# Up projection's transpose: from TensorE to transposing DMAs with 16-bit halves taken apart and put together on POOL

## Chip, core and metric

The kernel runs as one program on one core of a Trainium2 chip. The metric is the device time of one execution in microseconds. A core has five engines that each run their own list of instructions in order: PE (TensorE, matrix products and transposes), ACT (ScalarE), DVE (VectorE), POOL (GpSimd) and SP (SyncE, which here issues DMAs). Sixteen DMA engines move data between HBM and the on-chip memory SBUF, and within SBUF. PE writes its results to a second on-chip memory, PSUM.

## What is computed

One layer of a decoder trunk, for 256 tokens of width 2048 in fp32. Mixed state-space and attention heads come first, then a feed-forward part, then a gated embedding. The change lies in the feed-forward part:

```python
u = _rmsnorm(h, ffn_norm_g[i]) @ w_up[i]            # 256 x 2048 times 2048 x 11264
u = _causal_dwconv(u, ffn_conv_w[i], ffn_conv_b[i]) # 3 taps along the tokens, per feature
g_ff, u_ff = jnp.split(u, [D_FF], axis=-1)          # D_FF = 5632
h = h + (jax.nn.silu(g_ff) * u_ff) @ w_down[i]
```

The convolution runs along the tokens, each feature with its own three weights and bias.

## The kernel before

**Products.** All large products have the same shape. `gemm` (line 221) walks over loads of 128 x 1024 weights (two slices of 128 input features by 512 output features, 512 KB). `load_w` (line 196) loads one with a DMA on SP's queue (line 205) into one of five buffers `w`; `split` (line 188) makes a high part `wh` with a cast on ACT (line 190) and the remainder `wl` with a subtraction on DVE (line 191), each into one of four buffers. `products` (line 209) then issues, for each of the two slices and each of the two blocks of 128 tokens, three matmuls of 128 x 128 by 512 (lines 217 to 219: high by high, high by low, low by high), so 12 matmuls for a load; in the last load of a product all of the first block of tokens comes first. The result, two PSUM tiles `acc` of 128 tokens x 512 features, comes from a ring of two pairs.

**Up projection.** `up(c)` (line 769) computes 512 features from eight loads. ACT evicts both `acc` tiles with the tokens' norm factor as scale into `u` (line 775; one tile per block of tokens, two buffers each). In `u` tokens lie on the partitions, while the convolution wants features there and tokens along the row. So `conv_chunk` (line 270) transposes: for each of four groups of 128 features and each of two token blocks PE multiplies a 128 x 128 piece by the identity (line 277), eight transposes per call, into PSUM tiles `tr`. `conv_tile` (line 261) then writes the last tap and the bias with ACT (line 264) and adds the two other taps with DVE (line 266), from `tr` into `cv`, an SBUF tile of 128 features x 4 x 256 tokens. `conv_chunk` has other callers in the state-space part; they keep it.

**Feed-forward loop.** 22 calls of `up`, in segments of pairs: `SEGS = [2, 2, 2, 2, 2, 1]`. For each pair: `up` for the gate, SiLU on it (ACT, line 789), `up` for the other half, the product of both on POOL (line 791), and a split of it into `gh` and `gl` (ACT and DVE, lines 190 and 191), which is the stationary operand of the down projection. After each segment `project` (line 371) runs the down projection of the segment before (four groups of 512 output features, two loads per pair each), and DVE adds its result to the residual (line 357). So a segment's `gT` is read by PE only after the next segment's up projections, and for the last segment after the down projection of the one before.

**Order of the work.** No order is written by hand. The program is traced in the order of the code, and a scheduler puts each engine's instructions into a fixed list at build time, playing through a timeline (`schedule_with_timeline_sim=True`, line 884). On the chip each engine runs its list in order and stops at the first instruction whose semaphore isn't there. DMAs that are issued from ACT stand in ACT's list.

Of the kernel before, what the change touches and what calls it, by code (L numbers as in the profile page):

```python
# [11 lines left out]
F32 = mybir.dt.float32  # L12
F32R = mybir.dt.float32r
I32 = mybir.dt.int32
AF = mybir.ActivationFunctionType
ALU = mybir.AluOpType
AX = mybir.AxisListType
# [2 lines left out]
P = 128  # L20
T = 256
# [4 lines left out]
NC = 512  # L26
# [38 lines left out]
def hybrid_layer(  # L65
# [20 lines left out]
    nc = tc.nc  # L86
    V, S, G, PE = nc.vector, nc.scalar, nc.gpsimd, nc.tensor
# [12 lines left out]
    def nm(s):  # L100
        uid[0] += 1
        return f"{s}_{uid[0]}"
# [2 lines left out]

    def sb(pool, shape, tag, dt=F32, bufs=None):
        kw = {} if bufs is None else {"bufs": bufs}
        size = math.prod(shape[1:]) * (2 if dt == mybir.dt.bfloat16 else 4)
        tags = sizes.setdefault(pool.id, {})
        tags[tag] = max(tags.get(tag, 0), -(-size // 32) * 32 * (bufs or pool.bufs))  # L110
        return pool.tile(shape, dt, tag=tag, name=nm(tag), **kw)
# [10 lines left out]
    def tr_tile():  # L122
        return ps_tr.tile([P, NC], F32, tag="tr", name=nm("tr"))
# [14 lines left out]
    def load_first(k, pieces=1):  # L138

        xt = sb(xin, [P, T], "xt", bufs=6)  # L140
        nc.sync.dma_start(xt, xT[:, k, :])
        w = sb(wp, [P, KW, NC], "w", bufs=WR)
        n = KW // pieces
        for c in range(0, KW, n):
            cs = slice(c, c + n)
            nc.sync.dma_start(w[:, cs, :], w_in[cs, k // KW, :, (k % KW) * NC : (k % KW + 1) * NC].rearrange("c p n -> p c n"))
        return w, xt
# [30 lines left out]
    g_attn, g_ffn, g_ple, g_ssm = (gn[:, i * KT : (i + 1) * KT] for i in range(4))  # L178
    posi = sb(const, [P, NB], "posi", I32)

    def rstd(ss, n, cols, tag):
        t = sb(small, [P, cols], "rs_t")
        V.tensor_scalar(t, ss, 1.0 / n, EPS, op0=ALU.mult, op1=ALU.add)
        r = sb(small, [P, cols], tag)
        G.tensor_tensor(out=r, in0=t, in1=nhalf[:, :cols], op=ALU.pow)
        return r

    def split(src, hi, lo, scale=None):
# [3 lines left out]
        else:  # L192
            S.activation(out=hi, in_=src, func=AF.Copy, scale=scale)
            V.scalar_tensor_tensor(out=lo, in0=src, scalar=scale, in1=hi.bitcast(F32), op0=ALU.mult, op1=ALU.subtract)
# [48 lines left out]
    def transpose_split(src, lhs, k0, gain=None):  # L243

        for half in range(2):
            tr = tr_tile().rearrange("p (a t) -> p a t", a=2)
            for i in range(2):
                f = half * 2 + i
                for b in range(NB):
                    PE.transpose(tr[:, i, b * P : (b + 1) * P], src[b][:, f * P : (f + 1) * P], ident)  # L250
            k = k0 + half * 2
            if gain is None:
                h, l = lhs.t[k // KG]
                j = k % KG
                split(tr, h[:, j : j + 2, :], l[:, j : j + 2, :])
            else:
                for i in range(2):
                    h, l = lhs.part(k + i)
                    split(tr[:, i, :], h, l, gain[:, k + i : k + i + 1])

    def conv_tile(ps, dst, taps, bias):

        n = len(taps)
        S.activation(out=dst, in_=ps, func=AF.Identity, scale=taps[n - 1], bias=bias)  # L264
        for s in range(1, n):
            V.scalar_tensor_tensor(  # L266
                out=dst[:, s:], in0=ps[:, : T - s], scalar=taps[n - 1 - s], in1=dst[:, s:], op0=ALU.mult, op1=ALU.add
            )

    def conv_chunk(src, dst, cw, ntap, c0):  # L270

        for half in range(2):
            tr = tr_tile().rearrange("p (a t) -> p a t", a=2)
            for i in range(2):
                f = half * 2 + i
                for b in range(NB):
                    PE.transpose(tr[:, i, b * P : (b + 1) * P], src[b][:, f * P : (f + 1) * P], ident)  # L277
            for i in range(2):
                f = half * 2 + i
                w = cw[:, (c0 + f) * (ntap + 1) : (c0 + f + 1) * (ntap + 1)]  # L280
                conv_tile(tr[:, i, :], dst[:, f, :], [w[:, j : j + 1] for j in range(ntap)], w[:, ntap : ntap + 1])
# [14 lines left out]
    with xin_:  # L296
        wd = sb(xin, [P, KT, 32], "wd")
        dhl = sb(xin, [P, KT, 64], "dhl", F32R)
        for k in range(KT):
            w, xt = first[k] if k < len(first) else load_first(k)  # L300
# [23 lines left out]
            if k in (5, 9):  # L324
                b = k // 4 - 1
                nc.sync.dma_start(hres[b], x[b])
                xs = sb(xin, [P, D], "xs")
                S.activation(out=xs, in_=hres[b], func=AF.Square, accum_out=ssx[:, b : b + 1])
        rx_ = rstd(ssx, D, NB, "rx_")
# [16 lines left out]
    def evac_scaled(acc, pool, tag, bufs=None):  # L346
        res = []
        for b in range(NB):
            t = sb(pool, [P, NC], f"{tag}{b}", bufs=bufs)
            S.activation(out=t, in_=acc[b], func=AF.Copy, scale=rx[:, b : b + 1])  # L350
            res.append(t)
        return res
# [6 lines left out]
    def next_lhs(lhs, ss, n, gain):  # L359

        for b in range(NB):
            sq = sb(small, [P, NC], "hsq")
            S.activation(out=sq, in_=hres[b][:, n * NC : (n + 1) * NC], func=AF.Square, accum_out=ss[:, b, n : n + 1])
        transpose_split([hres[b][:, n * NC : (n + 1) * NC] for b in range(NB)], lhs, 4 * n, gain)
# [17 lines left out]
    with tc.tile_pool(name="ssd", bufs=1) as sp, tc.tile_pool(name="dram", bufs=1, space=bass.MemoryType.DRAM) as dp:  # L382
        BT = sb(sp, [P, 4, T], "BT")
        CT = sb(sp, [P, 4, T], "CT")
        for c, (acc, dst) in enumerate(((acc_b, BT), (acc_c, CT))):
            t = evac_scaled(acc, sp, "ct", 1)
            conv_chunk(t, dst, scw, 4, 16 + 4 * c)
            S.activation(out=dst, in_=dst, func=AF.Silu)

# [9 lines left out]
        dt = sb(sp, [P, 64], "dt")  # L399
# [128 lines left out]
        with tc.tile_pool(name="rope", bufs=1) as rp:  # L528
# [3 lines left out]
            for j in range(HALF):  # L532
                f = float(np.float32(THETA) ** np.float32(-2.0 * j / ROPE))
# [62 lines left out]
    with tc.tile_pool(name="att_s", bufs=2) as as_, tc.tile_pool(name="att", bufs=2, reuse_waits="tile") as ap_:  # L596
# [5 lines left out]
        def norm_rope(acc, b, gain, tag):  # L602
            r = sb(ap_, [P, NC], "qkr", bufs=1)
            S.activation(out=r, in_=acc[b], func=AF.Copy, scale=rx[:, b : b + 1])
            n = sb(ap_, [P, NC], "qkn")
            S.activation(out=n, in_=r, func=AF.Square)
            ss = sb(as_, [P, 8], "ss8")
            V.tensor_reduce(out=ss, in_=v3(n, 8), axis=AX.X, op=ALU.add)
            rs = rstd(ss, HD, 8, "rs8")
            V.tensor_tensor(out=v3(r, 8), in0=v3(r, 8), in1=bc(rs, HD), op=ALU.mult)  # L610
            G.tensor_tensor(out=v3(n, 8), in0=v3(r, 8), in1=gain.unsqueeze(1).to_broadcast([P, 8, HD]), op=ALU.mult)
            n3 = v3(n, 8)
            a, c_ = n3[:, :, :HALF], n3[:, :, HALF:ROPE]
            cs = cos_t[:, b, :].unsqueeze(1).to_broadcast([P, 8, HALF])
            sn = sin_t[:, b, :].unsqueeze(1).to_broadcast([P, 8, HALF])
            t = [sb(as_, [P, 8, HALF], f"rot{i}", bufs=1) for i in range(4)]
            for i, (u_, w_) in enumerate(((a, cs), (c_, sn), (c_, cs), (a, sn))):
                G.tensor_tensor(out=t[i], in0=u_, in1=w_, op=ALU.mult)
            G.tensor_tensor(out=a, in0=t[0], in1=t[1], op=ALU.subtract)
            G.tensor_tensor(out=c_, in0=t[2], in1=t[3], op=ALU.add)  # L620
            return n
# [88 lines left out]
        for b in range(NB):  # L710
            n = norm_rope(acc, b, kg_, "k")
# [31 lines left out]
    fcw = sb(pp, [P, 88 * 4], "fcw")  # L743
# [23 lines left out]
    with tc.tile_pool(name="ffn", bufs=2) as fp:  # L767

        def up(c):
            acc = acc_pair()  # L770
            gemm(acc, hT, [w_up[c, g] for g in range(KT // KW)])
            t = []
            for b in range(NB):
                u_ = sb(fp, [P, NC], f"u{b}")
                S.activation(out=u_, in_=acc[b], func=AF.Copy, scale=rh[:, b : b + 1])
                t.append(u_)
            cv = sb(fp, [P, 4, T], f"cv{c // NPAIR}")
            conv_chunk(t, cv, fcw, 3, 4 * c)
            return cv

        pair = 0
        pending = []
        ssg = sb(small, [P, NB, 4], "ssg", bufs=1)

        for s, np_ in enumerate(SEGS):
            gT = Lhs(fp, KG * np_, "g")
            for i in range(np_):
                cg = up(pair + i)
                S.activation(out=cg, in_=cg, func=AF.Silu)
                cu = up(NPAIR + pair + i)  # L790
                G.tensor_tensor(out=cg, in0=cg, in1=cu, op=ALU.mult)  # L791
                split(cg, gT.t[i][0], gT.t[i][1])
            if pending:
                project(*pending.pop())
            pending.append((gT, w_down, pair, np_))
            pair += np_
        h2T = Lhs(act, KT, "a")
        project(*pending.pop(), lambda n: next_lhs(h2T, ssg, n, g_ple))
        embed()
# [88 lines left out]
```

## Time and profile before

| | us |
|---|---|
| median of three runs | 1484.79 |
| lowest and highest | 1484.22 and 1485.33 |
| the profiled execution | 1485.15 |
| its span, first to last instruction | 1483.4 |

The granted TensorE clock is 1.000 over the span. Busy time is given for PE (matmuls), PEld (PE's weight loads, which overlap PE), DVE, ACT and POOL. Matmuls are pipelined, so their durations overlap: the time of one is read from start to start. A row of a group of instructions gives line, engine, operation, output and inputs by name, shapes and count, then total busy time and mean ns of one, then the idle time of the engine ahead of them and what ended it. A row of the timeline gives start, length, engine, line and operation; in brackets stands the idle time ahead of it and what ended it. A row that ends in x2 or x4 merges neighbours. A row of the waits gives who waited for whom, us in total, times, and the longest. For one line, durations are given as min/median/max in ns.

### The profile page before, as it was taken

How to read it: one execution, taken by the hardware profiler on the slowest of the kernel's cores; microseconds unless marked ns; L12 is line 12 of the kernel's file. 1: busy time of each engine (PE TensorE's matmuls, PEld its weight loads, DVE VectorE, ACT ScalarE, POOL GpSimd, SP SyncE). 2: the span in 40 equal slices, each digit the busy share in tenths (PEclk: the TensorE clock that was granted, in tenths of full speed). 3: DMA queues.
4: the chain of work that ended last, by engine and by line, in shares of the span. 5: the costliest groups of instructions: out<-in, count | busy, mean ns of one | idle time of the engine just before them, and what ended most of it. 6: DMA issues, size and time to landing. Idle time of an engine off the chain costs nothing.

```text
span 1483.4 us, 18448 instructions
## 1 busy us (share of the span) xinstructions
PE 1472.3 (99%) x6836; PEld 1198.2 (81%) x6836; DVE 970.7 (65%) x1288; ACT 795.2 (54%) x1103; POOL 122.5 (8%) x120
## 2 busy tenths in 40 slices
PE   9999999999999999999999999999999999999998
PEld 6787888888777777788888888888888888888887
DVE  6668876756758687766556646565665556566854
ACT  6575555545555554566555545544543554454643
POOL 0002010024033030000000000000000000000000
PEclk9999999999999999999999999999999999999999
DMA  9665665655555555466666666666666666666673
GB/s 324 198 195 177 206 189 161 182 155 172 156 156 148 165 147 159 133 194 201 183 187 186 186 193 183 187 192 192 180 192 191 182 194 186 187 190 188 205 225 98
DMA packets 79433, 271.65 MB, mean 183 GB/s; under 512 B 9008, under 2 KB 11888, under 8 KB 78960
## 3 DMA queue, kind: packets, MB, share of 16 engines
q1 hardware_dynamic: 78912, 270.01, 60.1%
q8 instruction: 53, 0.87, 0.3%
q10 hardware_dynamic: 432, 0.48, 0.1%
q14 instruction: 36, 0.29, 0.1%
HBM read 268.32 MB, written 2.13 MB: 182 GB/s over the span
## 4 chain that ended last, share of the span: by engine, by line
PE 93%; DMA 2%; DVE 2%; POOL 1%; ACT 1%; issue 1%; SPq 0%; DVEq 0%; POOLq 0%; ACTq 0%
PE acc L218 28%; PE acc L217 28%; PE acc L219 28%; PE tr L277 2%; PE ms L644 1%; DMA h<-in_x_dram 1%; PE ms L493 1%; PE ms L685 1%; PE tr L677 1%; DVE wl L191 1%; PE tr L250 1%; DMA wd<-in_w_dt_dram 1%; PE acc L316 0%; PE acc L317 0%; DMA seg<-scr 0%
## 5 line engine op out<-in xcount | busy, mean ns | idle before, releaser
L191 DVE TENSOR_TENSOR wl<-w,wh 128x1024 fp32r<-128x1024 f32 (+1 forms) x493 | 612.1, 1244 | 395.7 <-ACT wh L190 394.4
L190 ACT CAST wh<-w 128x1024 fp32r<-128x1024 f32 (+1 forms) x493 | 516.6, 1049 | 483.4 <-PE acc L219 405.8
L218 PE MATMUL acc<-wl,ah 128*128 128x512 f32 x1280 | 501.1, 392 | 1.5 <-DVE wl L191 1.4
L219 PE MATMUL acc<-wh,al 128*128 128x512 f32 x1280 | 500.7, 393 | 0.0
L217 PE MATMUL acc<-wh,ah 128*128 128x512 f32 x1280 | 500.1, 392 | 0.0
L218 PEld LDWEIGHTS acc<-wl,ah 128*128 128x128 f32 x1280 | 240.4, 188 | 52.8 <-DVE wl L191 2.3
L217 PEld LDWEIGHTS acc<-wh,ah 128*128 128x128 f32 x1280 | 240.5, 188 | 49.8 <-issue 1.6
L219 PEld LDWEIGHTS acc<-wh,al 128*128 128x128 f32 x1280 | 240.0, 188 | 49.2 <-issue 0.8
L219 PE MATMUL acc<-wh,gl 128*128 128x512 f32 x352 | 137.6, 391 | 0.0
L217 PE MATMUL acc<-wh,gh 128*128 128x512 f32 x352 | 137.4, 390 | 0.0
L218 PE MATMUL acc<-wl,gh 128*128 128x512 f32 x352 | 137.2, 390 | 0.0
L217 PE MATMUL acc<-wh,yh 128*128 128x512 f32 x256 | 101.0, 397 | 0.0
L218 PE MATMUL acc<-wl,yh 128*128 128x512 f32 x256 | 100.7, 393 | 0.0
L219 PE MATMUL acc<-wh,yl 128*128 128x512 f32 x256 | 100.5, 394 | 0.0
L791 POOL TENSOR_TENSOR cv<-cv,cv 128x1024 f32<-128x1024 f32 x11 | 35.5, 3230 | 649.2 <-DVE cv L266 649.2
L266 DVE SCALAR_TENSOR_TENSOR cv<-tr,fcw,cv 128x254 f32<-128x254 f32 (+1 forms) x176 | 73.9, 476 | 19.8 <-ACT cv L264 19.8
L357 DVE TENSOR_TENSOR h<-h,acc 128x512 f32<-128x512 f32 x112 | 73.7, 680 | 11.1 <-PE acc L219 11.1
L218 PEld LDWEIGHTS acc<-wl,gh 128*128 128x128 f32 x352 | 66.1, 188 | 13.5
L219 PEld LDWEIGHTS acc<-wh,gl 128*128 128x128 f32 x352 | 66.1, 188 | 13.5
L217 PEld LDWEIGHTS acc<-wh,gh 128*128 128x128 f32 x352 | 66.1, 188 | 13.4
L264 ACT ACTIVATE cv<-tr,fcw 128x256 f32<-128x256 f32 x88 | 44.8, 559 | 34.3 <-PE tr L277 34.3
L217 PEld LDWEIGHTS acc<-wh,yh 128*128 128x128 f32 x256 | 48.1, 188 | 12.1 <-issue 2.1
(229 smaller groups left out, 1095.2 us busy)
## 6 DMA issues: line engine op xcount, KB each, us to landing
w<-in_w_up_dram SPq DMA_DIRECT2D x176, 512.0 KB, 3.9
w<-in_w_in_dram SPq DMA_DIRECT2D x126, 512.0 KB, 3.9
w<-in_w_down_dram SPq DMA_DIRECT2D x88, 512.0 KB, 3.7
w<-in_w_out_dram SPq DMA_DIRECT2D x64, 512.0 KB, 3.7
w<-in_w_pg_dram SPq DMA_DIRECT2D x32, 512.0 KB, 4.2
seg<-scr SPq DMA_DIRECT2D x8, 512.0 KB, 6.0
xt<-in_xT_dram SPq DMA_DIRECT2D x16, 128.0 KB, 7.3
h<-in_x_dram SPq DMA_DIRECT2D x2, 1024.0 KB, 8.2
```

Of the source, the lines that this page charges most:

```text
L190: S.copy(hi, src)
L191: V.tensor_tensor(out=lo, in0=src, in1=hi.bitcast(F32), op=ALU.subtract)
L217: PE.matmul(acc[b], lhsT=hi, rhs=wh[:, i, :], start=(k == 0), stop=False)
L218: PE.matmul(acc[b], lhsT=hi, rhs=wl[:, i, :], start=False, stop=False)
L219: PE.matmul(acc[b], lhsT=lo, rhs=wh[:, i, :], start=False, stop=(k == total - 1))
L250: PE.transpose(tr[:, i, b * P : (b + 1) * P], src[b][:, f * P : (f + 1) * P], ident)
L264: S.activation(out=dst, in_=ps, func=AF.Identity, scale=taps[n - 1], bias=bias)
L266: V.scalar_tensor_tensor(out=dst[:, s:], in0=ps[:, : T - s], scalar=taps[n - 1 - s], in1=dst[:, s:], op0=ALU.mult, op1=ALU.add)
L277: PE.transpose(tr[:, i, b * P : (b + 1) * P], src[b][:, f * P : (f + 1) * P], ident)
L357: V.tensor_tensor(out=hs, in0=hs, in1=acc[b], op=ALU.add)
L493: PE.matmul(yp[:, hs], lhsT=segs[c][:, h, :], rhs=Xd[c][:, hs], start=True, stop=True)
L791: G.tensor_tensor(out=cg, in0=cg, in1=cu, op=ALU.mult)
```

## The change

`up` no longer calls `conv_chunk`. For each block of 128 tokens, ACT evicts `acc` into `u` as before. POOL copies `u`, read as 16-bit numbers, into `half`: first the 512 low halves of all features, then the 512 high halves. A transposing DMA, issued on ACT's queue, flips `half` (128 tokens x 1024) into `flip` (128 x 8 x 128 tokens: four groups of features of the one half, four of the other). POOL copies `flip` into `uc`, alternating low and high half, so that `uc` holds fp32 again, features on the partitions and 256 tokens along the row. `conv_tile` reads `uc` from SBUF in place of `tr` from PSUM. `half`, `flip` and `uc` have one buffer each; together they take 2 x 2 KB, 2 x 2 KB and 4 KB of each partition.

```diff
@@ helpers @@
+U16 = mybir.dt.uint16
...
-        size = math.prod(shape[1:]) * (2 if dt == mybir.dt.bfloat16 else 4)
+        size = math.prod(shape[1:]) * (2 if dt in (mybir.dt.bfloat16, U16) else 4)
@@ def up(c): @@
             acc = acc_pair()
             gemm(acc, hT, [w_up[c, g] for g in range(KT // KW)])
-            t = []
+            uc = sb(fp, [P, 4, T], "uc", bufs=1)
             for b in range(NB):
                 u_ = sb(fp, [P, NC], f"u{b}")
                 S.activation(out=u_, in_=acc[b], func=AF.Copy, scale=rh[:, b : b + 1])
-                t.append(u_)
+                half = sb(fp, [P, 2 * NC], f"half{b}", U16, 1)
+                G.tensor_copy(half.rearrange("p (a n) -> p a n", a=2), u_.bitcast(U16).rearrange("p (n a) -> p a n", a=2))
+                flip = sb(fp, [P, 8, P], f"flip{b}", U16, 1)
+                nc.scalar.dma_start_transpose(flip, half)
+                G.tensor_copy(
+                    uc[:, :, b * P : (b + 1) * P].bitcast(U16).rearrange("p f (t a) -> p f t a", a=2),
+                    flip.rearrange("p (a f) t -> p f t a", a=2),
+                )
             cv = sb(fp, [P, 4, T], f"cv{c // NPAIR}")
-            conv_chunk(t, cv, fcw, 3, 4 * c)
+            for f in range(4):
+                w = fcw[:, (4 * c + f) * 4 : (4 * c + f + 1) * 4]
+                conv_tile(uc[:, f, :], cv[:, f, :], [w[:, j : j + 1] for j in range(3)], w[:, 3:4])
             return cv
```

## The prediction

> **What bounds the kernel now.** I read the page first: engine shares, then the chain that ended last.
>
> ```profile
> span 1483.4 us, 18448 instructions
> PE 1472.3 (99%) x6836; PEld 1198.2 (81%) x6836; DVE 970.7 (65%) x1288; ACT 795.2 (54%) x1103; POOL 122.5 (8%) x120
> ...
> PE 93%; DMA 2%; DVE 2%; POOL 1%; ACT 1%; issue 1%; SPq 0%; DVEq 0%; POOLq 0%; ACTq 0%
> ```
>
> PE is the bound: 93% of the chain, and only 11.1 us of the span without it. A busy PE need not be well fed, so the next view is who waited for whom, for PE alone:
>
> ```profile
> PE acc L315 <- ACT wh L190: 1.5, 3, 1.1
> PE acc L218 <- DVE wl L191: 1.4, 1, 1.4
> PE tr L277 <- ACT ct L350: 1.3, 1, 1.3
> PE ms L153 <- PEq L878: 0.8, 1, 0.8
> PE tr L630 <- POOL qkn L620: 0.4, 1, 0.4
> ```
>
> These waits (us in total, times, longest) come to 5.4 us in the whole run, one of them (1.4 us) for a weight's low part; none is for the up projections' transposes. So time comes off this kernel by taking work off PE, and goes onto it by letting PE wait. What the change touches, from the groups by line and shape:
>
> ```profile
> L277 PE MATMUL tr<-ident,u 128*128 128x128 f32 x176 | 26.3, 272 | 0.0
> L190 ACT CAST wh<-w 128x1024 fp32r<-128x1024 f32 x491 | 515.4, 1051 | 481.1 <-PE acc L219 405.8 <-issue 30.8 <-ACT cv L264 18.0
> L191 DVE TENSOR_TENSOR wl<-w,wh 128x1024 fp32r<-128x1024 f32 x491 | 610.7, 1246 | 394.2 <-ACT wh L190 393.0
> L264 ACT ACTIVATE cv<-tr,fcw 128x256 f32<-128x256 f32 x88 | 44.8, 559 | 34.3 <-PE tr L277 34.3
> L266 DVE SCALAR_TENSOR_TENSOR cv<-tr,fcw,cv 128x255 f32<-128x255 f32 x88 | 39.6, 479 | 19.8 <-ACT cv L264 19.8
> L775 ACT ACTIVATE u<-acc,rh 128x512 f32<-128x512 f32 x44 | 30.3, 690 | 22.4 <-PE acc L219 22.4
> L791 POOL TENSOR_TENSOR cv<-cv,cv 128x1024 f32<-128x1024 f32 x11 | 35.5, 3230 | 649.2 <-DVE cv L266 649.2
> ```
>
> The important row is the cast: ACT idles 405.8 us until PE gives a weight buffer back. The weight supply runs as far ahead as its four buffers allow, and that lead is what any new delay on ACT or DVE eats first.
>
> **What it removes.** 176 transposes. Their 272 ns overlap each other, so 176 x 0.272 = 48 us is too much (even their busy total, 26.3 us, shares time with matmuls). I take the price from the pace. ACT rows of the timeline, the first evictions of two successive up projections and the convolution between them, and PE rows, the first of 25 matmuls in a stretch without transposes and the last:
>
> ```profile
> 680.74 0.69 ACT L775 ACTIVATE u<-acc,rh 128x512 f32<-128x512 f32 x1 [0.31 <-PE acc L219]
> ...
> 687.44 1.02 ACT L264 ACTIVATE cv<-tr,fcw 128x256 f32<-128x256 f32 x2 [1.57 <-PE tr L277]
> ...
> 703.45 0.69 ACT L775 ACTIVATE u<-acc,rh 128x512 f32<-128x512 f32 x1 [0.31 <-PE acc L219]
> ...
> 697.13 0.39 PE L217 MATMUL acc<-wh,ah 128*128 128x512 f32 x1
> 702.57 0.39 PE L217 MATMUL acc<-wh,ah 128*128 128x512 f32 x1
> ```
>
> Period 703.45 - 680.74 = 22.71 us. A matmul takes 5.44 / 24 = 0.2267 us, and an up projection has 8 loads x 12 = 96 of them: 21.76 us. So eight transposes cost 0.95 us (0.119 us each), and 22 calls give **-20.9 us** if PE waits for nothing new. That is the ceiling of the gain.
>
> **What it adds on the shared side of DVE and POOL.** Per call POOL gets four copies of 1024 16-bit elements per partition: two that take u apart, two that put the flipped halves together. No POOL copy of that kind is in the trace. The nearest rows, min/median/max in ns:
>
> ```profile
> L446 POOL TENSOR_SCALAR_AFFINE_SELECT seg<-seg x8: 1091/1913/2017, 112.3 to 253.6; 128x1024 f32<-128x1024 f32 x8
> L611 POOL TENSOR_TENSOR qkn<-qkr,qgs x8: 1269/1290/2136, 325.8 to 544.0; 128x512 f32<-128x512 f32 x8
> L618 POOL TENSOR_TENSOR rot<-qkn,cos x20: 313/323/1298, 328.0 to 547.7; 128x64 f32<-128x64 f32 x20
> ```
>
> One input, 1024 elements, undisturbed: 1.09 us. Two inputs: (1.269 - 0.313) / 448 = 2.13 ns an element, so 0.313 + 960 x 0.00213 = 2.36 us for 1024. Yet the product at L791 took 3.23 us, and the medians above sit near 1.9. Why, the timeline of POOL and DVE shows around one L791:
>
> ```profile
> 692.62 3.23 POOL L791 TENSOR_TENSOR cv<-cv,cv 128x1024 f32<-128x1024 f32 x1 [53.15 <-DVE cv L266]
> ...
> 692.37 1.21 DVE L191 TENSOR_TENSOR wl<-w,wh 128x1024 fp32r<-128x1024 f32 x1
> 695.06 1.87 DVE L191 TENSOR_TENSOR wl<-w,wh 128x1024 fp32r<-128x1024 f32 x1 [1.48 <-ACT wh L190]
> 698.11 1.22 DVE L191 TENSOR_TENSOR wl<-w,wh 128x1024 fp32r<-128x1024 f32 x1
> ```
>
> POOL starts under a DVE subtraction that ends at 693.58; 2.27 us more bring it to its end at 695.85, its own 2.36 us nearly. The subtraction that starts at 695.06 ends at 696.93, 1.08 us behind POOL's end. The two excluded each other. [...]
>
> So DVE and POOL must be added up. [...] Three periods of up projection, and one stretch of down projection, by the busy table (length, then PE, PEld, DVE, ACT, POOL, then granted clock, DMA share, GB/s):
>
> ```profile
> 681.43:704.14 22.71, 22.71 (x105) 18.81 (x104) 14.67 (x18) 12.58 (x15) 3.23 (x1) 1.00 0.64 188
> 704.14:726.85 22.71, 22.71 (x105) 18.81 (x104) 12.89 (x17) 12.70 (x15) 0.00 (x0) 1.00 0.63 189
> 726.85:749.60 22.75, 22.75 (x106) 18.82 (x105) 14.71 (x18) 12.58 (x16) 3.26 (x1) 1.00 0.64 180
> ...
> 820.00:862.00 42.00, 42.00 (x191) 34.79 (x190) 27.62 (x31) 18.70 (x20) 3.23 (x1) 1.00 0.64 190
> ```
>
> DVE: mean 14.1 us, less 0.65 blocked in two of three, 13.7 us. L791 is there every second call: 1.2 us. For taking apart (read in steps of 4 bytes, written in order) I take the one-input row, 1.1 us, bounds 1.1 and 1.9. Putting together reads from two places 1 KB apart in turn; bounds 1.1 and 2.4, and I take the middle, 1.7, as it has one input but a worse pattern. Sum: 13.7 + 1.2 + 2 x 1.1 + 2 x 1.7 = **20.5 us** of the 21.76 us in which PE does its work. It fits, barely; at the upper bounds 13.7 + 1.2 + 3.8 + 4.8 = 23.5 it doesn't. At the lower ones it is 19.3.
>
> **What it adds on ACT and the DMA engines.** Two transposing DMAs per call, on ACT's queue. Rows of plain transfers:
>
> ```profile
> 634.77 0.34 ACTq L744 DMA_DIRECT2D fcw<-in_ffn_cw_dram  x1
> ...
> pe<-in_pT_dram ACTq DMA_DIRECT2D x1, 256.0 KB, 5.2
> ...
> scr<-acsT SPq DMA_DIRECT2D x1, 32.0 KB, 2.4
> ```
>
> Landing: 5.2 us, the row of the same size (bounds 2.4 and, for a slow form, twice 5.2). Issue: 0.34 us of ACT, upper bound that of an issue that holds ACT until it has landed, 5.2. At 0.34 ACT goes from 12.6 to 13.3 us of 21.76. Traffic: 2 x 256 KB beside 8 x 512 KB of weights, at a DMA share of 0.64: it becomes about 0.72, and the weights' five buffers cover that.
>
> The chain from eviction to convolution: 0.7 evict, 0.6 mean lock wait, 1.1 apart, 0.34 + 5.2 DMA, 0.6 + 1.7 together = 10.2 us, and 1.4 later for the second half: 11.6 us. Today the convolution starts 6.7 us behind the eviction (687.44 - 680.74). Nobody is pressed by those 5 us: the next eviction is 21.76 us away, so single buffers do, and behind the last up projection comes a two-pair down projection of 192 matmuls, 43.5 us, before the last gT is read.
>
> What is pressed is queued behind. ACT issues a transpose only when POOL has taken u apart; behind that wait stand the casts, and behind a late convolution, on ACT and on DVE, stand casts and subtractions. Their lead:
>
> ```profile
> 702.09 1.05 ACT L190 CAST wh<-w 128x1024 fp32r<-128x1024 f32 x1 [1.67 <-PE acc L219]
> 703.17 1.23 DVE L191 TENSOR_TENSOR wl<-w,wh 128x1024 fp32r<-128x1024 f32 x1 [1.50 <-ACT wh L190]
> ```
>
> PE frees a buffer at 702.1, its refill is ready at 704.4, and PE gets there after three other loads of 12 matmuls, at 702.1 + 3 x 2.72 = 710.3. **The lead is 5.9 us.** A POOL operation takes at most 2.4 of it, a wait for POOL on ACT 1 to 2. The lead should hold, and the trace has no price for the rest; I let two of the six segments end in one wait of PE like the 1.4 us of the first view: **+2.8 us**, an estimate with bounds 0 and 11 (half a us in each call).
>
> **Sum.** 1485.15 (the profiled run: span 1483.4 and 1.75 around it) - 20.9 + 2.8 = 1467.05. The median of the runs is 0.36 us lower; I forecast 1467.0. Own range of this case: 1463 (all of the gain, 1464.2, less the runs' spread) to 1475 (the 11 us).
>
> **Rival 1: the port saturates.** If the four copies average over (21.76 - 14.9) / 4 = 1.7 us, DVE and POOL together set the pace. At the upper bounds, 23.5 us, a call takes 1.7 us longer than PE needs. Without relief that is 22 x 23.5 in place of 22 x 22.71: 1485.15 + 17.4 = 1502.5. A segment begins with its lead of 5.9 us restored, though (in the stretch of down projection DVE has 14.4 of 42 us free), and four calls lose 6.8: of 37 us, up to 6 x 5.9 come back, which would give 1466. Mutual waits spend lead too; I take half, 1485. For it: L446's median of 1.9. Against it: its minimum of 1.09. [...]
>
> **Rival 2: slower, through ACT's order.** ACT runs its list in the order fixed at build. If issue and landing are longer than that order allows for, ACT stands at the transpose's issue or at the convolution, the casts behind it come late, and once that exceeds 5.9 us PE stops. It decides from about 6 us on: issues of 3 us or more, or a landing near 10. Each us beyond costs 22; at 2 us beyond, 1485.15 - 20.9 + 44 = 1508. For it: no transposing DMA in this trace, and a wait on a busy POOL ahead of it. Against: the 5.2 us row, and ACT's 9 us idle per call. [...]
>
> **How the numbers follow.** Forecast 0.52, rival 1 0.26, rival 2 0.22. About 0.2% (3 us) is what a measurement of this kernel can tell from no change. The forecast case is faster but for 0.01; rival 1 is spread from 1466 to 1502: faster 0.06, same 0.08, slower 0.12; rival 2 is slower but for 0.02 within the bound. Faster 0.57, same 0.11, slower 0.32. The range, 1463 to 1508, holds the forecast (0.51), rival 1 (0.25) and the nearer part of rival 2 (0.08).
>
> **What would show it.** Right: no rows of L277 on u; first evictions 21.8 us apart; POOL copies at 1.1 to 2 us; casts still waiting for PE; PE's waits a few us in all. Wrong by rival 1: copies of 2 us and more, subtractions stretched to 2 us and over all along, PE waiting for wl late in each segment. Wrong by rival 2: ACT idle ahead of L264 for a DMA or a POOL copy, or transposes holding ACT's queue for us, and PE waiting for wh just behind each eviction. A PE pace of other than 0.2267 us would break the first term.

## The result and the profile after

The changed kernel takes 1466.63 us (median of four runs, 1463.53 to 1470.42), the kernel before beside it 1484.92 (1484.22 to 1485.33). The ratio is 0.9879, with 95% between 0.9864 and 0.9895: 18.3 us faster, where 17.8 had been forecast. One thing doesn't look like the kernel before: its four runs lie within 1.1 us, those of the changed kernel 6.9 us apart. (In later rounds the runs of the kernel before spread over 3 to 4 us, those of the changed kernel over 14.)

The profiled execution is the slowest of the four (1470.42 us). Its page:

```profile
span 1468.7 us, 18308 instructions
PE 1454.3 (99%) x6660; PEld 1183.1 (81%) x6660; DVE 990.3 (67%) x1288; ACT 790.7 (54%) x1103; POOL 245.8 (17%) x208
...
PE 91%; DMA 3%; DVE 2%; POOL 1%; issue 1%; ACT 1%; SPq 0%; DVEq 0%; ACTq 0%; POOLq 0%
```

PE has 176 matmuls fewer (6660 for 6836), POOL 88 copies more (208 for 120) and twice the busy time. PE still bounds the kernel, but the chain now has 3% of DMA in it. The first evictions of three successive up projections on ACT (start, length, instruction, idle time ahead of it and what ended that) show the pace:

```profile
903.18 0.69 ACT L776 ACTIVATE u<-acc,rh 128x512 f32<-128x512 f32 x1 [0.31 <-PE acc L220]
...
924.94 0.69 ACT L776 ACTIVATE u<-acc,rh 128x512 f32<-128x512 f32 x1 [0.30 <-PE acc L220]
...
946.70 0.69 ACT L776 ACTIVATE u<-acc,rh 128x512 f32<-128x512 f32 x1 [0.30 <-PE acc L220]
```

The period is 21.76 us, 96 matmuls of 0.2267 us to the hundredth, in place of 22.71. (Lines have moved: what was L190, L191, L217 to L219, L264, L266, L775 and L791 is now L191, L192, L218 to L220, L265, L267, L776 and L801.) The new operations, by line (min/median/max in ns, first and last start), and the time from issue to landing of the transposing DMAs:

```profile
L778 POOL COPY half<-u x44: 1030/1040/2470, 660.4 to 1297.9; 128x1024 uint16<-128x1024 uint16 x44
L780 ACTq DMA_TRANSPOSE flip<-half x44: 1246/1249/2517, 663.0 to 1302.5; - x44
...
DMA to landing us min/median/max: 2.8/6.2/17.9
```

```profile
L781 POOL COPY uc<-flip x44: 1153/1164/2199, 668.3 to 1310.1; 128x1024 uint16<-128x1024 uint16 x44
```

Undisturbed, a copy takes 1.04 us (taking apart) or 1.16 us (putting together); the maxima, 2.47 and 2.20 us, are copies that stood behind a DVE subtraction (POOL from 1209.78 and 1197.43, DVE to 1211.35 and 1198.61). A landing takes 6.2 us in the median and 17.9 at the worst. What each engine waited for (us in total, times, longest), PE first, then ACT at the convolution:

```profile
PE acc L218 <- ACT wh L191: 3.3, 1, 3.3
PE acc L219 <- DVE wl L192: 2.6, 3, 1.3
```

```profile
ACT cv L265 <- POOL uc L781: 29.2, 12, 10.0
```

In 12 of 22 calls ACT stood at the convolution until POOL had put the halves together, 29.2 us in all. PE stood for more than half a us behind one of these, the longest.

**That one call.** ACT around it, then POOL, then PE from the last matmul ahead of the hole to the first at full pace:

```profile
764.97 0.69 ACT L776 ACTIVATE u<-acc,rh 128x512 f32<-128x512 f32 x1 [0.30 <-PE acc L220]
...
769.11 1.29 ACTq L780 DMA_TRANSPOSE flip<-half  x1
771.82 1.05 ACT L191 CAST wh<-w 128x1024 fp32r<-128x1024 f32 x1 [1.71 <-PE acc L220]
771.89 1.37 ACTq L780 DMA_TRANSPOSE flip<-half  x1
...
779.93 1.06 ACT L191 CAST wh<-w 128x1024 fp32r<-128x1024 f32 x1 [1.67 <-PE acc L220]
790.99 2.07 ACT L265 ACTIVATE cv<-uc,fcw 128x256 f32<-128x256 f32 x4 [10.00 <-POOL uc L781]
792.97 1.98 ACT L191 CAST wh<-w 128x1024 fp32r<-128x1024 f32 x2
```

```profile
779.87 1.16 POOL L781 COPY uc<-flip 128x1024 uint16<-128x1024 uint16 x1 [11.52 <-DMA flip<-half]
789.80 1.15 POOL L781 COPY uc<-flip 128x1024 uint16<-128x1024 uint16 x1 [8.76 <-DMA flip<-half]
```

```profile
790.39 0.39 PE L220 MATMUL acc<-wh,al 128*128 128x512 f32 x1
794.04 0.53 PE L218 MATMUL acc<-wh,ah 128*128 128x512 f32 x1 [3.27 <-ACT wh L191]
795.85 0.80 PE L219 MATMUL acc<-wl,ah 128*128 128x512 f32 x1 [1.28 <-DVE wl L192]
796.45 0.63 PE L220 MATMUL acc<-wh,al 128*128 128x512 f32 x1
...
800.71 0.63 PE L218 MATMUL acc<-wh,ah 128*128 128x512 f32 x1
...
801.41 0.39 PE L220 MATMUL acc<-wh,al 128*128 128x512 f32 x1
```

The two DMAs, issued 2.8 us apart, landed 10.6 and 17.9 us after their issue. POOL put the second half together at once (it had idled 8.76 us), ACT stood at the convolution for 10.0 us, and the two casts behind it in its list came only at 792.97. Read load by load, the weights of the first of them had landed at 782.52, so it was the order of ACT's list that held it. Its lead, 5.9 us by the prediction, was used up, and PE stood for 3.27 and 1.28 us. Then it ran at half pace: ten matmuls from 796.45 to 800.71, 0.426 us each. The busy table says why (length, then PE, PEld, DVE, ACT, POOL, granted clock, DMA share, GB/s):

```profile
785.00:790.00 5.00, 5.00 (x24) 4.14 (x23) 0.00 (x0) 0.00 (x0) 0.20 (x1) 1.00 0.82 219
790.00:795.00 5.00, 1.30 (x5) 0.50 (x3) 3.37 (x8) 4.01 (x7) 0.95 (x1) 0.94 0.29 118
795.00:800.00 5.00, 4.15 (x10) 3.28 (x11) 3.46 (x4) 2.03 (x3) 3.38 (x1) 0.50 0.56 143
800.00:805.00 5.00, 5.00 (x21) 4.06 (x20) 3.20 (x3) 3.94 (x4) 2.65 (x3) 0.88 0.81 228
770.00:775.00 5.00, 5.00 (x24) 4.14 (x23) 2.45 (x2) 1.67 (x3) 0.00 (x0) 1.00 1.04 87
780.00:785.00 5.00, 5.00 (x24) 4.14 (x23) 1.23 (x1) 0.99 (x1) 1.03 (x1) 1.00 1.34 171
```

Behind the wait of 3.27 us the granted clock is 0.50 for a window, where it was 1.00 ahead. By the runs below the length of a single wait doesn't settle it: waits of 2.09 and 1.26 us close together were followed by 0.50 too (one DMA per call, 1319.30 and 1321.61), and one of 2.54 us left the clock at 1.00 (every transposing DMA twice, 1120.37). In all, 15 matmuls started behind 790.39 and up to 801.41; at full pace they take 3.4 us and they took 11.0. The call cost 7.6 us, and 1470.42 - 7.6 = 1462.8 is an estimate of what this execution would have taken without it.

The last two rows of the table lie ahead of the hole, while the transposes were under way. The DMA engines count as full (a share of 1.04 and 1.34) and move only 87 and 171 GB/s. The weights suffered with them; the DMA issues of 762 to 792 us (count, KB each, median us to landing), beside 4.1 us for these loads over the whole run:

```profile
w<-in_w_up_dram SPq DMA_DIRECT2D x8, 512.0 KB, 11.3
flip<-half ACTq DMA_TRANSPOSE x2, 14.2
```

### The profile page after: what moved, and what is told of

Read it like the earlier page. It is cut to its first block, busy times and chain, and to the rows that moved or that the text cites. A ratio compares the mean times of both kernels' runs of the same rounds, so it can differ in the third digit from the quotient of the medians.

```text
span 1468.7 us, 18308 instructions
## 1 busy us (share of the span) xinstructions
PE 1454.3 (99%) x6660; PEld 1183.1 (81%) x6660; DVE 990.3 (67%) x1288; ACT 790.7 (54%) x1103; POOL 245.8 (17%) x208
## 3 DMA queue, kind: packets, MB, share of 16 engines
q10 hardware_dynamic: 46896, 12.02, 5.6%
## 4 chain that ended last, share of the span: by engine, by line
PE 91%; DMA 3%; DVE 2%; POOL 1%; issue 1%; ACT 1%; SPq 0%; DVEq 0%; ACTq 0%; POOLq 0%
PE acc L219 27%; PE acc L218 27%; PE acc L220 27%; DMA flip<-half 2%; PE ms L645 1%; PE acc L317 1%; PE ms L494 1%; PE acc L318 1%; PE acc L316 1%; PE ms L686 1%; DVE wl L192 1%; PE tr L678 1%; PE tr L251 1%; DVE cv L267 0%; POOL rs L186 0%
## 5 line engine op out<-in xcount | busy, mean ns | idle before, releaser
L192 DVE TENSOR_TENSOR wl<-w,wh 128x1024 fp32r<-128x1024 f32 (+1 forms) x493 | 628.0, 1279 | 345.3 <-ACT wh L191 344.1
L191 ACT CAST wh<-w 128x1024 fp32r<-128x1024 f32 (+1 forms) x493 | 514.8, 1048 | 481.8 <-PE acc L220 419.7
L219 PE MATMUL acc<-wl,ah 128*128 128x512 f32 x1280 | 501.7, 392 | 2.6 <-DVE wl L192 2.6
L218 PE MATMUL acc<-wh,ah 128*128 128x512 f32 x1280 | 499.2, 392 | 3.3 <-ACT wh L191 3.3
L220 PE MATMUL acc<-wh,al 128*128 128x512 f32 x1280 | 499.7, 392 | 0.0
L218 PEld LDWEIGHTS acc<-wh,ah 128*128 128x128 f32 x1280 | 241.0, 188 | 54.8 <-ACT wh L191 3.7
L219 PEld LDWEIGHTS acc<-wl,ah 128*128 128x128 f32 x1280 | 241.1, 188 | 54.3 <-DVE wl L192 3.7
L220 PEld LDWEIGHTS acc<-wh,al 128*128 128x128 f32 x1280 | 240.6, 188 | 50.1 <-issue 0.8
L219 PE MATMUL acc<-wl,gh 128*128 128x512 f32 x352 | 137.0, 389 | 0.0
L220 PE MATMUL acc<-wh,gl 128*128 128x512 f32 x352 | 137.0, 389 | 0.0
L218 PE MATMUL acc<-wh,gh 128*128 128x512 f32 x352 | 136.4, 389 | 0.0
L778 POOL COPY half<-u 128x1024 uint16<-128x1024 uint16 x44 | 59.7, 1371 | 257.6 <-ACT u L776 257.6
L218 PE MATMUL acc<-wh,yh 128*128 128x512 f32 x256 | 101.0, 397 | 0.0
L219 PE MATMUL acc<-wl,yh 128*128 128x512 f32 x256 | 100.7, 393 | 0.0
L220 PE MATMUL acc<-wh,yl 128*128 128x512 f32 x256 | 100.5, 394 | 0.0
L781 POOL COPY uc<-flip 128x1024 uint16<-128x1024 uint16 x44 | 62.0, 1411 | 197.2 <-DMA flip<-half 180.4
L267 DVE SCALAR_TENSOR_TENSOR cv<-uc,fcw,cv 128x254 f32<-128x254 f32 (+1 forms) x176 | 75.0, 483 | 22.2 <-ACT cv L265 22.1
L220 PEld LDWEIGHTS acc<-wh,gl 128*128 128x128 f32 x352 | 66.1, 188 | 13.7
L219 PEld LDWEIGHTS acc<-wl,gh 128*128 128x128 f32 x352 | 66.1, 188 | 13.6
L218 PEld LDWEIGHTS acc<-wh,gh 128*128 128x128 f32 x352 | 66.1, 188 | 13.6
L265 ACT ACTIVATE cv<-uc,fcw 128x256 f32<-128x256 f32 x88 | 45.8, 591 | 29.2 <-POOL uc L781 29.2
```

Of the source, the lines that this page charges most:

```text
L191: S.copy(hi, src)
L192: V.tensor_tensor(out=lo, in0=src, in1=hi.bitcast(F32), op=ALU.subtract)
L218: PE.matmul(acc[b], lhsT=hi, rhs=wh[:, i, :], start=(k == 0), stop=False)
L219: PE.matmul(acc[b], lhsT=hi, rhs=wl[:, i, :], start=False, stop=False)
L220: PE.matmul(acc[b], lhsT=lo, rhs=wh[:, i, :], start=False, stop=(k == total - 1))
L267: V.scalar_tensor_tensor(out=dst[:, s:], in0=ps[:, : T - s], scalar=taps[n - 1 - s], in1=dst[:, s:], op0=ALU.mult, op1=ALU.add)
```

## The experiments

Three causes were to be told apart: the transposes' price on PE, the waits of DVE and POOL for each other (rival 1's port), and the DMAs, which land late and hold ACT (rival 2's mechanism, in single calls). For the last there were two versions. By theory C, transposes are slow when two of them are in flight together; by theory E, what counts is how much transposing traffic falls into a short time beside the weight loads, whether in one DMA or in two. All times are medians, in us; "landing" is min/median/max from issue to landing in the profiled execution.

| kernel | us (runs from, to) | ratio to before, 95% | landing |
|---|---|---|---|
| changed, again | 1467.58 (1463.52 to 1477.36) | 0.9896 (0.9869 to 0.9922) | 2.7/6.4/14.9 |
| no transposition | 1464.14 (1462.85 to 1464.86) | 0.9861 (0.9848 to 0.9874) | none |
| addition only, beside PE's transposes | 1485.12 (1483.76 to 1486.44) | 1.0002 (0.9994 to 1.0011) | 4.3/5.2/6.1 |
| convolution behind next eviction | 1464.36 (1463.52 to 1465.70) | 0.9864 (0.9850 to 0.9878) | 2.7/4.7/8.8 |
| plain DMA | 1464.09 (1463.39 to 1464.57) | 0.9856 (0.9841 to 0.9871) | 2.5/4.7/6.0 |
| every POOL copy twice | 1474.11 (1473.67 to 1474.68) | 0.9924 (0.9908 to 0.9941) | 2.7/5.8/8.5 |
| every transposing DMA twice | 1532.05 (1522.48 to 1539.03) | 1.0310 (1.0266 to 1.0353) | 2.8/6.9/19.3 |
| DMAs kept apart | 1463.99 (1462.69 to 1464.86) | 0.9855 (0.9840 to 0.9870) | 2.7/5.3/6.9 |
| DMAs from SP's queue | 1463.73 (1463.05 to 1464.44) | 0.9856 (0.9841 to 0.9870) | 4.1/5.3/8.4 |
| one DMA per call | 1469.62 (1463.11 to 1472.35) | 0.9886 (0.9857 to 0.9915) | 4.6/8.6/17.2 |

**The changed kernel again**, to see whether the wide spread returns.

> The changed kernel once more, unaltered, to see how far its executions spread. Theory (late landing): the gain of 20.9 us is whole in most executions, 1463 to 1465, and a transposing DMA that lands late costs one execution in two or three some 3 to 8 us, up to about 1471; the spread is then several times the 1.1 us of the kernel before. Rival (DVE and POOL exclude each other): the price is paid in every call alike, so executions lie within 1.5 us of each other, about 1466 to 1467.

Six runs lie between 1463.52 and 1477.36. PE's waits of the profiled one (1468.34 us):

```profile
PE acc L219 <- DVE wl L192: 4.3, 7, 1.3
...
PE acc L218 <- ACT wh L191: 0.3, 1, 0.3
```

The spread is the kernel's own. Here ACT stood at the convolution 40.1 us in all, at most 7.0 at a time; PE's waits stay at 1.3 us or less, and the granted clock is 1.00. So in these two traces late landings cost little while ACT's stand is near the lead, and much when it is well beyond it. All ten runs of the changed kernel have a median of 1467.6.

**No transposition at all**: the convolution reads `u` as it is, and the POOL copies and the DMAs are left out too.

```diff
-            uc = sb(fp, [P, 4, T], "uc", bufs=1)
+            t = []
...
-                nc.scalar.dma_start_transpose(flip, half)
...
+                t.append(u_)
...
-                conv_tile(uc[:, f, :], cv[:, f, :], [w[:, j : j + 1] for j in range(3)], w[:, 3:4])
+                conv_tile(t[f // 2][:, (f % 2) * T : (f % 2 + 1) * T], cv[:, f, :], [w[:, j : j + 1] for j in range(3)], w[:, 3:4])
```

> Leaves the transposes out altogether: no POOL copies, no transposing DMAs, and the convolution reads u untransposed, so the features are mixed up with tokens. It is the ceiling of the gain. Theory: 1485.1 less 20.9 is 1464, with a spread of about 1 us, and the best executions of the changed kernel lie as low as this. Rival (port, or ACT's issues of 1.25 us): this one lies below the best executions of the changed kernel by 2 us or more.

1464.14 us, 20.5 below the kernel before at its side (1484.61): the transposes' price on PE, where 20.9 had been worked out from the pace. This is the ceiling, and the changed kernel lies some 3 us above it.

**The addition alone**: PE keeps its transposes, and POOL's copies and the DMAs run beside them for nothing.

```diff
+            t = []
...
+                t.append(u_)
...
-            for f in range(4):
-                w = fcw[:, (4 * c + f) * 4 : (4 * c + f + 1) * 4]
-                conv_tile(uc[:, f, :], cv[:, f, :], [w[:, j : j + 1] for j in range(3)], w[:, 3:4])
+            conv_chunk(t, cv, fcw, 3, 4 * c)
```

> The additions alone: PE transposes and the convolution as before, and beside them the POOL copies and the transposing DMAs, whose result nobody reads. Theory (late landing): nobody waits for the flipped data, so this is 1484 to 1487, narrow. Rival (port, issues): what POOL and ACT are made to do costs PE in any case: 1488 or more.

1485.12 us beside 1484.61: no difference that can be measured. In this arrangement copies, issues and traffic that nobody waits for cost nothing. It doesn't test late landings, since there are none here:

```profile
DMA to landing us min/median/max: 4.3/5.2/6.1
```

**The convolution queued behind the next call's eviction**, on ACT and DVE, with two buffers of `uc`. Nothing is taken away; a landing has a whole call more time.

```diff
-            uc = sb(fp, [P, 4, T], "uc", bufs=1)
+            uc = sb(fp, [P, 4, T], "uc", bufs=2)
...
+            if later:
+                with tc.issue_after(evicted.ins):
+                    later.pop()()
...
+            later.append(conv)
```

> The same work as the changed kernel, but each call's convolution (and what follows it on ACT) is queued in ACT's list behind the next call's eviction, with two uc buffers, so a landing may be some 20 us late before ACT stands. Theory (late landing): 1463 to 1465 in all executions, a spread of 1 to 1.5 us, PE's waits for wh and wl gone. Rival (port): as the changed kernel, 1466 to 1467. Rival (a longer chain costs elsewhere): slower than the changed kernel.

1464.36 us, the ceiling, within 2.2 us over its runs. PE's waits for the weights:

```profile
PE acc L219 <- DVE wl L192: 1.3, 2, 1.1
```

ACT doesn't wait at the convolution at all. The time is what the theory of late landings expects, but the run doesn't show by itself that a late landing costs nothing in this order: its longest is 8.8 us. The edit also moved the DMAs against the weight loads. In 11 of the 22 calls the two DMAs are 2.6 to 2.7 us apart, as close as in the changed kernel, and land in 6.3 us at most; but in the first 3 us behind the first DMA only one weight load is issued in 21 calls, where the changed kernel has two in 14. That the 3 us come through ACT's order rests on the trace of the late call above. The copies that put together took 2.38 us on average here, twice the undisturbed time, and the ceiling is reached all the same.

**A plain DMA** of the same bytes in place of the transposing one.

```diff
-                nc.scalar.dma_start_transpose(flip, half)
+                nc.scalar.dma_start(flip, half.rearrange("p (a t) -> p a t", a=8))
```

> The two transposing DMAs per call become plain DMAs of the same 256 KB between the same tiles on the same queue; the features come out mixed with tokens. Theory A (the transposing form makes landings late): landing near the 5 us of a plain 256 KB transfer in every call, no late ones, 1463 to 1465. Theory B (any added traffic beside the weight loads does it): landings spread as in the changed kernel, 2.7 to 15 us, and 1464 to 1471.

1464.09 us. Its landings, and the DMA queue line of its page, then that of the changed kernel (packets, MB, share of 16 engines):

```profile
L780 ACTq DMA_DIRECT2D flip<-half x44: 472/472/518, 664.8 to 1296.0; - x44
...
DMA to landing us min/median/max: 2.5/4.7/6.0
```

```profile
q10 hardware_dynamic: 6768, 12.01, 2.4%
```

```profile
q10 hardware_dynamic: 46896, 12.02, 5.6%
```

The same 12 MB, in a seventh of the packets and under half of the engines' time, land by 6.0 us without exception, and are issued in 0.47 us instead of 1.25. The DMAs of a call are 2.7 to 4.3 us apart, and two weight loads fall into the first 3 us in 14 calls, as in the changed kernel. So the form differs, and with it the issue; the shorter issue isn't what brings the time down, since the version with its DMAs kept apart (below) reaches the ceiling with issues of 1.25 us. Late landings belong to the transposing form: (46,896 - 432) / 44 = 1056 packets per DMA, some 250 bytes each (432 packets were on this queue before).

**Every POOL copy twice**, on the version with the late convolution, so that rival 1 is tested without ACT standing at the convolution.

```diff
+                G.tensor_copy(sb(fp, [P, 2 * NC], "spare", U16, 1).rearrange("p (a n) -> p a n", a=2), u_.bitcast(U16).rearrange("p (n a) -> p a n", a=2))
...
+                G.tensor_copy(
+                    sb(fp, [P, 4, 2 * P], "spare", U16, 1).rearrange("p f (t a) -> p f t a", a=2),
+                    flip.rearrange("p (a f) t -> p f t a", a=2),
+                )
```

> Rival 1 by itself: e3_behind with each of the four POOL copies done twice, the second time into a tile that nobody reads. Undisturbed copies take 1.04 and 1.16 us in the changed kernel, so four more add 4.4 us of POOL time per call: 13.7 + 1.2 + 8.8 = 23.7 us of DVE and POOL against 21.76 us of PE. If the two exclude each other, PE waits for wl in the up projections: 22 x 1.9 = 43 us, less up to 35 of lead that comes back, 1472 to 1507. If they don't, it stays within 2 us of e3_behind's 1464.4.

1474.11 us, 9.75 above the same kernel without the second copies. PE's waits:

```profile
PE acc L218 <- ACT gh L191: 3.8, 1, 3.8
PE acc L219 <- DVE wl L192: 3.0, 5, 1.5
```

DVE and POOL do hold each other up: subtractions took 1366 ns on average, against 1248 without the second copies. But even at twice the copies (some 8.8 us undisturbed per call) PE doesn't wait in each call. The 3.8 us stand at 1341.19 us, at the last segment's down projection, for which the chain through POOL, with the second copies in it, delivers the last product late; behind that wait matmuls start 0.43 us apart for some us (1341.78 to 1344.34), in place of 0.2267. In this order POOL may lag: the first DMAs of successive calls are spread over 22 to 37 us each, where the changed kernel has some 22 us and then a pause of 65, so POOL's copies run on into the down projections. Over a segment of four calls and a down projection there is room, by an estimate from the rows of the kernel before: 4 x 23.7 + 43.5 x 27.62 / 42.00 = 123 us of DVE and POOL in 130.5 us of PE. Rival 1's mechanism shows at twice the load, and its 1502 not even there; the run doesn't show what the doubled copies would cost where the convolution is not late.

**Every transposing DMA twice**, the second into a spare tile, which has one buffer for both blocks.

```diff
+                nc.scalar.dma_start_transpose(sb(fp, [P, 8, P], "spare", U16, 1), half)
```

> The changed kernel with each transposing DMA issued twice, the second time into a tile that nobody reads: twice the transposing traffic, 5 us of ACT's queue per call for issues in place of 2.5, same POOL copies. Theory (late landing): landings grow and late ones come in most calls, ACT stands at the convolution, PE stops: 1475 to 1520. Rival (landings have nothing to do with transposing traffic): within 3 us of the changed kernel.

1532.05 us, 47 above the kernel before, and above the range expected. Landings, and PE's waits:

```profile
DMA to landing us min/median/max: 2.8/6.9/19.3
```

```profile
PE acc L218 <- ACT wh L191: 26.7, 9, 7.6
PE acc L219 <- DVE wl L192: 10.3, 16, 1.3
```

The profiled execution (1522.48 us) lies 58.3 above the ceiling: 37.0 us of these waits, and at a mean granted clock of 0.986 some 0.014 x 1521 = 21 us of slow matmuls. 15 of the 44 landings in `flip` take over 9 us, 7 in the changed kernel. But most of the waits are not the late call of the changed kernel over again. What held ACT ahead of its casts, and its rows ahead of the longest wait of PE (7.6 us, up to 1223.08):

```profile
ACT wh L191 <- issue: 127.9, 31, 15.3
```

```profile
1203.29 2.19 ACTq L781 DMA_TRANSPOSE spare<-half  x1
...
1205.62 6.79 ACTq L780 DMA_TRANSPOSE flip<-half  x1
1220.61 1.25 ACTq L781 DMA_TRANSPOSE spare<-half  x1
1221.98 2.94 ACT L191 CAST wh<-w 128x1024 fp32r<-128x1024 f32 x3 [15.34 <-issue]
```

ACT stood for 127.9 us where the profile shows nothing but its own issues, in the changed kernel for 29.9. One issue took 6.8 us, and the second DMA into `spare` was issued only 17.3 us behind the first, when that had landed and the buffer was free. Four of the nine waits for `wh`, 17.7 of the 26.7 us, come straight behind such a stand; at the convolution ACT stood for 39.2 us. This is rival 2 by its other arm, ACT standing at the issue. The run shows that more transposing traffic makes more late landings and long issues; what the traffic would cost without the single buffer of `spare` it doesn't show.

**The two DMAs of a call kept apart**: POOL takes the second block apart only when it has put the first together, so that the issues are 8.2 to 11.6 us apart, mostly 10.9.

```diff
-                G.tensor_copy(half.rearrange("p (a n) -> p a n", a=2), u_.bitcast(U16).rearrange("p (n a) -> p a n", a=2))
+                with tc.issue_after(joined.ins) if b else ExitStack():
+                    G.tensor_copy(half.rearrange("p (a n) -> p a n", a=2), u_.bitcast(U16).rearrange("p (n a) -> p a n", a=2))
...
-                G.tensor_copy(
+                joined = G.tensor_copy(
```

> The changed kernel with one order added on POOL: the second block is taken apart only behind the putting together of the first, so its transposing DMA is issued when the first has landed and two are never in flight together. Theory C (late landings come from two transposes in flight beside a weight load): all landings below 7 us, and 1463 to 1466, though the chain to the convolution gets some 4 us longer. Theory D (a transpose beside weight loads is enough): landings up to 10 us and more stay, and with the longer chain the spread is at least that of the changed kernel, 1464 to 1477.

1463.99 us, the ceiling, in runs 2.2 us apart. Landings, and ACT's wait at the convolution:

```profile
DMA to landing us min/median/max: 2.7/5.3/6.9
```

```profile
ACT cv L265 <- POOL uc L782: 4.7, 4, 1.3
```

No landing exceeds 6.9 us, and no other queue was touched. This version beats both kernels: by 20.9 us the one before at its side (1484.93), and the changed one by 3.6 on the median of its ten runs.

**The DMAs issued from SP's queue.**

```diff
-                nc.scalar.dma_start_transpose(flip, half)
+                nc.sync.dma_start_transpose(flip, half)
```

> The changed kernel with both transposing DMAs issued from SP's queue, among the weight loads, in place of ACT's. Theory C: ACT is freed of the issues, but the two transposes still overlap each other and a load, so late landings and waits of ACT at the convolution stay: 1464 to 1477. Rival (ACT's queue, with its 1.25 us an issue, is what makes the late events): 1463 to 1465, narrow. A second rival (a transpose that waits for POOL holds the weight loads behind it): slower than the changed kernel, PE waiting for wh whose cast waits for a load.

1463.73 us: narrow and at the ceiling, which theory C did not expect. The longest landing is 8.4 us. It doesn't single out the queue, though: the scheduler also moved the two DMAs of a call further apart (mostly 4.1 to 4.9 us, against 1.5 to 2.8 in most calls of the changed kernel), and against the weight loads.

**One DMA of 512 KB per call**, so that two are never in flight.

```diff
-                nc.scalar.dma_start_transpose(flip, half)
+            nc.scalar.dma_start_transpose(flip, half.rearrange("p b n -> p (b n)"))
```

> One transposing DMA of 512 KB per call, issued when both blocks are taken apart, in place of two of 256 KB: the same traffic with never two in flight. Theory C (two in flight near a weight load make the late landings): the landing is about twice that of one, 8 to 11 us, and narrow; 1463 to 1466. Theory E (it is the amount of transposing traffic in a short time, in one DMA or in two): landings spread to 15 us and more, and 1465 to 1477 or worse.

1469.62 us, and the runs are spread again (1463.11 to 1472.35). Landings, and PE's wait:

```profile
L780 ACTq DMA_TRANSPOSE flip<-half x22: 1591/4856/6216, 667.2 to 1295.5; - x22
...
DMA to landing us min/median/max: 4.6/8.6/17.2
```

```profile
PE acc L219 <- DVE wl L192: 2.7, 2, 1.4
PE acc L218 <- ACT wh L191: 2.1, 1, 2.1
```

Theory C falls: a single transpose in flight lands nearly as late as the worst pair, and the weight loads beside that one (issues of 1290 to 1312 us) took 11.4 us. Here the late loads hold ACT too: it stood 7.07 us ahead of a cast at 1311.77 whose load, issued at 1295.86, landed at 1311.67, and then 3.42 us at the convolution.

Theory E is not refuted, but the traces show that the amount in a short time is not the whole condition. In the changed kernel's own trace, read DMA by DMA, the four calls whose DMAs are 4.2 to 4.3 us apart land in 3.8 to 7.6 us, and the long landings are all among the 18 whose distance is 1.5 to 2.8 us. Run again, however, it has a DMA issued 3.9 us behind the first, when that had just landed, and this one took 11.0 us (931.47); and with the later convolution pairs 2.6 us apart took 6.3 at most. The moment beside the weight loads differs between these versions as well, and no run varies it alone.

## Why the prediction was right, point by point

**What is removed.** Right, to 0.4 us: -20.9 worked out, -20.5 measured without any transposition, and the pace of 21.76 us as written down. Pricing the transposes by the pace was the step that mattered; by their mean duration they would have been put at 48 us.

**The shared side of DVE and POOL.** Right that it fits, and the sum was too high. The term for putting together, 1.7 us, was mis-sized: 1.16 undisturbed. Taking apart was 1.04 for 1.1. By these, 13.7 + 1.2 + 2 x 1.04 + 2 x 1.16 = 19.3 us, the prediction's lower end. That its pattern is worse was shown by no row before: the read that alternates between two places 1 KB apart took 12% longer than the one in steps of 4 bytes (1.16 us for 1.04). Rival 1 is thus too dear by its price, and the doubled copies, in an order where POOL may lag, cost 9.75 us and not the 22 x 1.9 of the plain sum: POOL's work runs on into the down projections. The prediction had allowed for such relief by half (its 1485 is 1484 by its own terms). The sum counts the convolution's taps among the work that POOL can't run beside; no run tests that by itself. With `tr` as source none took over 0.49 us; of the 176 from `uc` one took 1.26, beside a POOL copy (680.06), the median 0.48.

**Issue and landing.** Both mis-sized. An issue takes 1.25 us, not 0.34. That costs ACT nothing visible: its idle time ahead of casts that only issue explains is 29.9 us, where the kernel before had 30.8, and a cast that has started runs on beside the issue (771.82 and 771.89). What stands behind a long issue does wait, as the doubled DMAs show. Landing was put at 5.2 us with 10.4 as the bound of a slow form. The median is 6.2, and the bound fell: 17.9. The traffic was mis-sized as well: a DMA share of 0.72 was worked out from the bytes (0.75 with the shorter period), and 0.79 is measured from 903.18 to 946.70, as a transposing DMA keeps the engines busy for over twice the time of a plain one (5.6% for 2.4%). That the five weight buffers cover it failed in the late call, where weight loads took 11.3 us.

**The chain to the convolution.** Put at 11.6 us. By the same trace the first call's eviction starts at 659.63 and its convolution at 675.20, 15.6 us. The working left out that the two issues stand in ACT's list behind casts that wait for PE: they come 3.4 and 6.1 us behind the eviction, and the second landing then took 8.3. In the late call it was 26.0 us (764.97 to 790.99).

**The give-back**, +2.8 us. The size came out (3.5 us between the median of ten runs and the ceiling), but by luck: the prediction had no price for it, and the place was wrong. The prediction spread it as a 1.4 us wait for `wl` over two of six segments, each run alike. In fact it is 0 to 13 us from execution to execution: small waits in some, and in the profiled one a single call of 7.6 us by **rival 2's mechanism**, ACT standing at the convolution with the casts behind it. The signature that the prediction gave for that rival is there in part: ACT idle ahead of the convolution in 12 calls, and PE waiting for `wh` for long in one. The working failed in treating rival 2 as one price for all 22 calls ("each us beyond costs 22"), and in having no term for the slow clock behind a long wait, which made 3.1 of the 7.6 us (7.6 less 3.27 and 1.28). Its deciding point, a landing near 10 us, was somewhat early: landings are longer than that in three calls of the profiled execution and in six of the other traced one, and PE stood for more than 1 us at a time in one call of each. With every DMA issued twice, 1532 us is beyond rival 2's 1508, mostly by its other arm, ACT standing at an issue.

**Shown and open.** Shown: the gain is PE's; the rest comes with late landings, since plain DMAs in the same places bring the time to the ceiling; late landings belong to the transposing form; and in the call traced they reach PE through the order of ACT's list. Queueing the convolution later and spacing the DMAs both reach the ceiling, but both also move the DMAs against the weight loads, so the order and the moment are not told apart there. Open: what makes only some transposing DMAs late, why landings stay narrow beside PE's transposes although the DMAs lie 3.6 us apart there and overlap, and whether the SP queue itself helps. That the runs of 1474.72 and 1477.36 us had more such calls is likely, but they have no trace.

## What to carry to other kernels

Price what is taken off a saturated engine by the pace with and without it, not by the duration of its instructions. When a transfer takes over a step, the median landing is not enough: look for the longest one, and ask what stands behind its consumer in the consumer's list; then try that consumer behind something that is not urgent, and the transfers further apart. Here either brought the time to the ceiling. A wider spread of runs than before can be a sign of such a rare event, and here the trace of one of the longer runs shows it. When a run doubles something to test a cause, look also at what else the doubling makes wait, here a spare tile with one buffer.

## What the runs showed of the hardware

In the late call 512 KB weight loads beside two transposing DMAs took 11.3 us (median of eight) in place of 4.1, while the DMA engines counted as full and moved 87 and 171 GB/s in two stretches of 5 us. The same bytes by plain DMA in the same places landed by 6.0 us, with a median of 4.2 for the up projections' weight loads. With the transposing ones that median is 4.1 over the whole run; the weight loads issued from 1 us ahead of a call's first DMA to 10 us behind it took 6.7 us or less, in the median, in 18 of the 22 calls. And an issue of 512 KB in one transposing DMA held its queue for 1.6 to 6.2 us, 4.9 in the median, where 256 KB took 1.25 in the median: mostly more than in proportion. What stood behind it in ACT's list waited: an issue of 6.8 us is part of the 15.3 us for which ACT stood with every DMA issued twice.
